# A two-layer encoder: accumulating transfers for low parts, one later mean, x in four transfers with a reordered first norm

## The chip, the cores and the metric

One core of a Trainium2 chip runs the whole kernel. The metric is the device time of one execution in microseconds, from the first instruction to the last and what lies around them. The time before the change is 1551.14 us, the median of three runs (1551.08 to 1551.52).

The engines are TensorE (PE in the rows; PEld is its loading of weights), VectorE (DVE), ScalarE (ACT), GpSimd (POOL) and SyncE (SP), which here only issues transfers. ACTq and SPq are the queues on which ScalarE and SyncE issue transfers; POOL issues some as well, by instructions of its own.

## The reference

Two equal layers work on 512 tokens of 1024 values in float32; 256 memory tokens stand beside them.

```
mem_n = rms_norm(mem, mem_norm_g)
for l in range(DEPTH):                       # 2
    h = rms_norm(x, g_pre_mix[l])
    proj = h @ w_in[l]                       # 1024 -> 5632, split in q, k, v of three branches, and gates
    o_a = neighborhood_attention(q_a, k_a, v_a, rpb_na[l])   # a learned position bias
    o_b = dilated_attention(q_b, k_b, v_b)
    o_m = memory_attention(q_m, mem_n, w_mem_kv[l])
    merged = sum over the branches of sigmoid(gate + b_gate[l]) * (o @ w_br[l])
    x = x + rms_norm(merged @ w_out[l], g_post_mix[l])
    h = rms_norm(x, g_pre_ffn[l])
    a, b = split(depthwise_conv(h @ w_up[l]))
    x = x + rms_norm((gelu(a) * b) @ w_down[l], g_post_ffn[l])
```

## The kernel before

Activations stand with the channels on the 128 partitions and the tokens in the columns: x is eight tiles of 128 channels (k = 0 to 7), each in two halves of 256 tokens. Every float32 matrix product is made from three products of rounded numbers: a number is split into a high part (its value rounded to the type that TensorE takes at full rate) and a low part (what is left), and `mm3` adds high x high, high x low and low x high. So each weight that is loaded (`wraw`, by SP, 512 KB for a column of 1024 x 128) is turned into a high part by a cast on ScalarE and a low part by a subtraction on VectorE or POOL (`split`, L223 to L225). In the groups that this change is about, high and low parts are tiles `m` of 128x512, two of each for a column of weights. There are three raw buffers, so a load waits until the one three before it has been read.

The program of TensorE is written by a scheduler (`Woven`): jobs are generators that say with `yield` by how much work of TensorE their next step comes later, and TensorE's instructions go out in that order. The other engines get their instructions in the order in which the steps are run, and each engine works through its own list in order. So a `yield`, or the time at which a job is spawned, sets the place of all that the job issues, on every engine.

A norm is made by `rstd_job`: TensorE multiplies squares by a column of 1/1024 (`pt<-mean,...`, the mean), ScalarE takes a square root, VectorE the reciprocal, and TensorE spreads it over the partitions (`pt<-ident,st`). Then `normed` makes h for each k on VectorE (`h<-x,g,pt`), ScalarE casts its high part and VectorE subtracts the low part.

The start. x comes in eight transfers of 256 KB on SP; TensorE runs two products with zeros meanwhile (`idle(2)`). ScalarE squares half 0 (y<-x), VectorE adds the squares in pairs, four means follow, then h of half 0. The first six columns of w_in, the groups, are worked in pairs by `run_group`, half 0 first: pairs of groups 0 and 1 (`mm<-h,m`), 2 and 3 (`o` and `pt`), 4 and 5 (`s<-h,m x48`: eight k, three products, two groups), then the same for half 1. The low parts of groups 0, 1, 2 and 4 are VectorE's, those of 3 and 5 POOL's. The norm of half 1 is spawned at SD1 = 4.0 and that of the memory tokens (`mem_norm_job`: four loads `in_memT` on ScalarE's queue, squares on ScalarE) at 6.0. POOL also loads the position bias of a head (128 KB, `in_rpb`, into a `y` buffer) and subtracts it from three masks (`a_bias`, L596 and L599).

The passage from layer 0 to layer 1. While the last products of layer 0 end, `end_job` adds the normed result to x for half 0 (VectorE: y<-y,pt, then x<-x,y) and squares it (ScalarE: sq, VectorE: acc<-acc,sq), and the mean of acc gives layer 1 its first norm. `raw_end_job` does this for half 1, whose groups are multiplied with x before its norm is known; its own mean of squares comes 3.5 of TensorE's time after the last step. `kv_ahead` splits the weights for the keys and values of the memory (KVE, four columns) and of the first two groups (GEN[0], GEN[1]); the other four groups follow. In GEN and KVE, V is VectorE and G is POOL.

Of the kernel before, what the change touches and what calls it, by code (L numbers as in the profile page):

```python
# [37 lines left out]
SQG, LOG, GEN, KVE = {0: (), 1: ()}, {0: (), 1: ()}, 'GGVGVG', 'VVGG'  # L38
SD1 = 4.0
# [80 lines left out]
def tile_hybrid_encoder(ctx, tc, xT, memT, memg, vecs, rpb, w_in, w_kv, w_bra, w_brb, w_brm,  # L120
# [59 lines left out]
    DUP, MDUP = G, G  # L180
    MSQ = G
# [10 lines left out]
    def load_x(half):  # L192
        for k in range(0, KD, 2):
            i = half.start // 256
            nc.sync.dma_start(out=xs[:, i, k:k + 2, :], in_=xT[:, i, k:k + 2, :])
# [31 lines left out]
    def weights(src, K, C, slot=None, eng=None, after=None):  # L227

        raw = wp.tile([128, K, C], F32, tag="wraw", name=nm("wraw"))
        nc.sync.dma_start(out=raw, in_=src)  # L230
        if slot is None:
            hi = wp.tile([128, K, C], F32R, tag="whi", name=nm("whi"), bufs=2)
            lo = wp.tile([128, K, C], F32R, tag="wlo", name=nm("wlo"), bufs=2)
            split(raw, hi, lo, eng)
            behind(last_copy[0], after)
            return [(hi[:, k, :], lo[:, k, :]) for k in range(K)]
        n = 512 // C
        w = []
        for k in range(0, K, n):
            c = min(n, K - k)  # L240
            hi, lo = slot(F32R, (128, c, C)), slot(F32R, (128, c, C))
            split(raw[:, k:k + c, :], hi, lo, eng)
            w += [(hi[:, i, :], lo[:, i, :]) for i in range(c)]
        return w
# [81 lines left out]
    def rstd_job(accs, n, box):  # L326
# [4 lines left out]
        for i, a in enumerate(accs):  # L331
            for b in range(nb):
                mm(pt[:, b:b + 1], a[:, 128 * b:128 * b + 128], mean, i == 0 and b == 0,
                   i == len(accs) - 1 and b == nb - 1, 0.11)
        rs = smalls(nb)
        crit[0] = ACT.activation(rs, pt, AF.Sqrt, bias=eps, scale=1.0).ins
        V.reciprocal(rs, rs)
        yield 0.8
        for b in range(nb):
            one = rs[:, b:b + 1]  # L340
            spread = bass.AP(one.tensor, one.offset, [list(one.ap[0]), [0, 128]])
            wv.pe(nc.tensor.transpose(pr[:, 128 * b:128 * b + 128], spread, ident), 0.11)
        box.append(pr)
# [20 lines left out]
    def pre_norm_job(l, goff, acc, hs, i):  # L364
        half, box = HALVES[i], []
        yield from rstd_job(acc if isinstance(acc, list) else [acc[:, half]], 256, box)
# [51 lines left out]
    def raw_end_job(l, goff, og, acc, acc2, nxt, lat):  # L418
# [17 lines left out]
        yield 3.5  # L436
# [428 lines left out]
    def first_squares(half):  # L865
        sqs = [ytile((128, 256)) for _ in range(KD)]
        for k in range(KD):
            ACT.activation(sqs[k], xh(k, half), AF.Square)
# [8 lines left out]
    def idle(n):  # L877

        one, none = mean[:, 0:1], zero[:, 0:1]
        a, b = (bass.AP(t.tensor, t.offset, [list(t.ap[0]), [0, w]]) for t, w in ((one, 128), (none, 512)))  # L880
        for _ in range(n):
            mm(idle_bank, a, b, True, True, 0.0)
# [3 lines left out]
    wv.spawn(pre_norm_job(0, V_PRE, first_squares(HALVES[0]), hs, 0))  # L886
    gw = group_weights([w_in[0, m] for m in FIRST[:2]], (V, V))
# [7 lines left out]
    gw += group_weights([w_in[0, m] for m in FIRST[2:]], (V, G, V, G))  # L895
# [6 lines left out]
    for l in range(depth):  # L902
# [99 lines left out]
        else:  # L1002
# [10 lines left out]
            def kv_ahead(l=l, pre=pre, gw=gw):  # L1013
                pre.append(weights(w_kv[l + 1, 0], KD, 128, htile))
                yield KVD
                for i in (1, 2, 3):
                    yield 0.9
                    pre.append(weights(w_kv[l + 1, i], KD, 128, big, G if KVE[i] == 'G' else V))
                wv.give(f"kv{l + 1}")
                for m in range(NG):  # L1020
                    yield GWD
                    gw.extend(group_weights([w_in[l + 1, FIRST[m]]], [G if GEN[m] == 'G' else V]))
# [6 lines left out]
            gw += group_weights([w_in[l + 1, m] for m in FIRST[NG:]], [G if e == 'G' else V for e in GEN[NG:]])  # L1029
# [34 lines left out]
def _layout(inputs):  # L1064
# [13 lines left out]
    a["xT"] = np.ascontiguousarray(g["x"][0].T.reshape(KD, 128, 2, 256).transpose(1, 2, 0, 3))  # L1078
# [46 lines left out]
```

## Time and profile before

| | before |
|---|---|
| median of three runs | 1551.14 us |
| the profiled execution | 1551.73 us |
| its span, first to last instruction | 1550.0 us |
| TensorE busy | 1522.5 us (98%) |
| VectorE, ScalarE, POOL busy | 951.6, 712.7, 149.7 us |
| mean granted clock of TensorE | 0.995 |

All rows come from one profiled execution. The page gives the whole; TensorE's idle time is span less busy time. The list of waits says what TensorE waited for and on whom; the timeline shows one line for a run of equal instructions on an engine, with its start, duration and count, and in brackets the idle time before it and what ended it. The granted clock is the share of TensorE's full speed, 1.00 for 2.4 GHz and 0.50 for 1.2 GHz.

### The profile page before, as it was taken

To read this page: it belongs to the slowest core of one execution; us is meant where nothing else is said; L and a number is where in the kernel's file an instruction comes from. 1 tells how busy PE (TensorE), PEld (TensorE's weight loads), DVE (VectorE), ACT (ScalarE), POOL (GpSimd) and SP (SyncE) were. 2 spreads that over 40 slices of the span, in tenths; PEclk is the share of its full clock that TensorE was granted. 3 is DMA by queue.
4 is the path that set the end of the run, shared out by engine and by line. 5 is a ranking of instruction groups with operands and counts; after the bars stand their busy time and mean duration, and the time that the engine had idled before them with its cause. 6 is when DMAs were issued, how large, how long until landed. Compare 5 with 4: busy or idle time off the path is not lost.

```text
span 1550.0 us, 20648 instructions
## 1 busy us (share of the span) xinstructions
PE 1522.5 (98%) x7970; PEld 1300.1 (84%) x7970; DVE 951.6 (61%) x1684; ACT 712.7 (46%) x1266; POOL 149.7 (10%) x217
## 2 busy tenths in 40 slices
PE   8999999999999999999989999999999999999997
PEld 7988888888988888888888888888889888888887
DVE  6685676335777777742497756753456977776233
ACT  5565554336544444532355555532354544444231
POOL 3340000110000000000154300002100000000000
PEclk9999999999999999999999999999999999999999
DMA  7221213235113322333431221132350233323331
GB/s 246 89 88 64 62 57 107 84 95 165 53 59 100 100 96 95 118 90 101 129 102 59 78 66 58 61 104 88 102 177 15 82 96 99 101 99 89 99 105 63
DMA packets 45810, 144.91 MB, mean 93 GB/s; under 512 B 5376, under 2 KB 9600, under 8 KB 45712
## 3 DMA queue, kind: packets, MB, share of 16 engines
q1 hardware_dynamic: 43776, 139.85, 28.5%
q10 hardware_dynamic: 1296, 2.10, 0.4%
q0 software_dynamic: 640, 1.64, 0.3%
q8 instruction: 62, 1.02, 0.3%
q14 instruction: 36, 0.29, 0.1%
HBM read 141.48 MB, written 2.10 MB: 93 GB/s over the span
## 4 chain that ended last, share of the span: by engine, by line
PE 91%; DVE 6%; ACT 2%; issue 1%; DMA 0%; SPq 0%; ACTq 0%; DVEq 0%
PE mm L247 80%; PE s L247 4%; PE o L247 3%; PE pt L258 2%; DVE m L114 1%; DVE y L114 1%; PE pt L247 1%; DVE ka L114 1%; DVE x L114 1%; ACT y L114 1%; DVE st L114 0%; DVE acc L114 0%; DMA x<-in_xT_dram 0%; DVE wlo L114 0%; ACT whi L114 0%
## 5 line engine op out<-in xcount | busy, mean ns | idle before, releaser
L247 PE MATMUL mm<-h,whi 128*128 128x512 f32 x2496 | 776.5, 392 | 0.0
L247 PEld LDWEIGHTS mm<-h,whi 128*128 128x128 f32 x2496 | 462.0, 188 | 91.3
L247 PE MATMUL mm<-h,wlo 128*128 128x512 f32 x1248 | 486.9, 390 | 0.0
L114 DVE TENSOR_TENSOR wlo<-wraw,whi 128x1024 fp32r<-128x1024 f32 (+1 forms) x213 | 259.2, 1217 | 284.7 <-ACT whi L114 282.3
L114 ACT CAST whi<-wraw 128x1024 fp32r<-128x1024 f32 (+1 forms) x213 | 221.4, 1040 | 307.8 <-PE mm L247 293.4
L247 PEld LDWEIGHTS mm<-h,wlo 128*128 128x128 f32 x1248 | 234.5, 188 | 49.6
L247 PE MATMUL mm<-m,whi 128*128 128x512 f32 (+1 forms) x800 | 215.1, 356 | 1.0 <-DVE m L114 0.8
L247 PEld LDWEIGHTS mm<-m,whi 128*128 128x128 f32 x800 | 141.8, 189 | 22.8 <-PE mm L247 1.3
L247 PE MATMUL mm<-m,wlo 128*128 128x512 f32 (+1 forms) x400 | 142.1, 355 | 0.0
L114 DVE SCALAR_TENSOR_TENSOR y<-y,vec,y 128x511 f32<-128x511 f32 x176 | 130.5, 748 | 3.5 <-ACT y L114 0.9
L114 DVE TENSOR_TENSOR y<-mm,R 128x512 f32<-128x512 f32 x82 | 56.4, 688 | 68.5 <-PE mm L247 68.5
L247 PEld LDWEIGHTS mm<-m,wlo 128*128 128x128 f32 x400 | 75.5, 189 | 10.9
L802 POOL TENSOR_TENSOR m<-m,y 128x512 f32<-128x512 f32 x28 | 36.1, 1289 | 399.4 <-DVE y L114 399.4
L114 ACT ACTIVATE y<-y,vec 128x512 f32<-128x512 f32 x88 | 71.1, 815 | 2.3 <-DVE y L114 1.9
L247 PE MATMUL mm<-m,m 128*128 128x512 f32 x240 | 63.5, 394 | 0.0
L114 ACT ACTIVATE y<-y 128x512 f32<-128x512 f32 x44 | 27.9, 633 | 71.7 <-DVE y L114 71.3
L114 ACT CAST m<-pt 128x512 fp32r<-128x512 f32 (+1 forms) x72 | 38.6, 541 | 46.8 <-PE pt L258 38.5
L114 ACT ACTIVATE y<-y,st 128x256 f32<-128x256 f32 (+1 forms) x80 | 43.8, 549 | 30.4 <-DVE st L114 28.9
L114 DVE TENSOR_TENSOR acc<-acc,sq 128x256 f32<-128x256 f32 (+1 forms) x80 | 41.1, 514 | 26.6 <-ACT sq L114 24.7
L114 DVE TENSOR_TENSOR m<-pt,m 128x512 fp32r<-128x512 f32 (+1 forms) x72 | 45.1, 630 | 19.9 <-ACT m L114 18.6
L114 ACT CAST m<-y 128x512 fp32r<-128x512 f32 x32 | 19.9, 622 | 72.5 <-DVE y L114 72.5
L247 PE MATMUL mm<-h,m 128*128 128x256 f32 x312 | 49.1, 301 | 2.0 <-ACT h L114 1.0
(154 smaller groups left out, 1789.9 us busy)
## 6 DMA issues: line engine op xcount, KB each, us to landing
wraw<-in_w_in_dram SPq DMA_DIRECT2D x88, 512.0 KB, 3.7
wraw<-in_w_up_dram SPq DMA_DIRECT2D x88, 512.0 KB, 3.6
wraw<-in_w_down_dram SPq DMA_DIRECT2D x32, 512.0 KB, 3.5
wraw<-in_w_out_dram SPq DMA_DIRECT2D x16, 512.0 KB, 3.9
wraw<-in_w_down_dram SPq DMA_DIRECT2D x16, 384.0 KB, 3.1
wraw<-in_w_kv_dram SPq DMA_DIRECT2D x8, 512.0 KB, 4.0
wraw<-in_w_bra_dram SPq DMA_DIRECT2D x16, 192.0 KB, 2.3
x<-in_xT_dram SPq DMA_DIRECT2D x8, 256.0 KB, 7.3
```

The lines of the kernel that those rows point to most:

```text
L114: return op(*args, **kw)
L247: wv.pe(nc.tensor.matmul(ps, a, b, start=first, stop=last), cost)
L258: wv.pe(nc.tensor.transpose(ps[:, 128 * i:128 * i + 128], s, ident), 0.11)
L802: (V if br == 2 and m >= 6 else G).tensor_add(acc[m], acc[m], gs)
```

## The change

It has three parts.

First, a third way to make a low part, named D: ScalarE casts the high part as before, then writes minus the rounded value into the low part's tile, and POOL issues a transfer of 256 KB that reads the weight again from memory and adds it to what stands in the tile (L246 of the changed kernel). Sixteen tiles are made so: those of groups 4 and 5 in layer 0 (POOL had 3 and 5), and of the key-value columns 2 and 3 and groups 0, 1, 4 and 5 in layer 1 (POOL had the two columns, and groups 0, 1, 3 and 5). POOL makes no low parts of weights any more.

Second, the mean of half 1 in `raw_end_job` comes after 5.0 instead of 3.5 of TensorE's time.

Third, x comes in four transfers of 512 KB, 4 KB per partition. In the first norm VectorE makes two of the eight squares, `rstd_job` puts four short products with zeros between its steps (one after the second mean, one before the spreading, two behind it), the second group's weights are split after the norm's job is spawned, and SD1 becomes 5.0.

```diff
-SQG, LOG, GEN, KVE = {0: (), 1: ()}, {0: (), 1: ()}, 'GGVGVG', 'VVGG'
-SD1 = 4.0
+SQG, LOG, GEN, KVE = {0: (), 1: ()}, {0: (), 1: ()}, 'DDVVDD', 'VVDD'
+SD1 = 5.0
...
+    ENG = {'G': G, 'V': V, 'D': 'D'}
...
     def load_x(half):
-        for k in range(0, KD, 2):
+        for k in range(0, KD, 4):
             i = half.start // 256
-            nc.sync.dma_start(out=xs[:, i, k:k + 2, :], in_=xT[:, i, k:k + 2, :])
+            nc.sync.dma_start(out=xs[:, i, k:k + 4, :], in_=xT[i, k // 4])
...
             hi, lo = slot(F32R, (128, c, C)), slot(F32R, (128, c, C))
-            split(raw[:, k:k + c, :], hi, lo, eng)
+            if eng == "D":
+                last_copy[0] = ACT.copy(hi, raw[:, k:k + c, :]).ins
+                ACT.activation(lo, raw[:, k:k + c, :], AF.Copy, scale=-1.0)
+                nc.gpsimd.dma_start(out=lo, in_=src[:, k:k + c, :], accum_op=ALU.add)
+            else:
+                split(raw[:, k:k + c, :], hi, lo, eng)
...
-    def rstd_job(accs, n, box):
+    def rstd_job(accs, n, box, warm=None):
...
+            if warm and i == 1:
+                warm(1, 256)
         rs = smalls(nb)
         crit[0] = ACT.activation(rs, pt, AF.Sqrt, bias=eps, scale=1.0).ins
         V.reciprocal(rs, rs)
+        if warm:
+            warm(1, 256)
         yield 0.8
...
+        if warm:
+            warm(2, 256)
         box.append(pr)
...
-        yield 3.5
+        yield 5.0
...
-            ACT.activation(sqs[k], xh(k, half), AF.Square)
+            if half == HALVES[0] and k in (3, 7):
+                V.tensor_mul(sqs[k], xh(k, half), xh(k, half))
+            else:
+                ACT.activation(sqs[k], xh(k, half), AF.Square)
...
-    def idle(n):
+    def idle(n, w=512):
...
-    wv.spawn(pre_norm_job(0, V_PRE, first_squares(HALVES[0]), hs, 0))
-    gw = group_weights([w_in[0, m] for m in FIRST[:2]], (V, V))
+    sqs = first_squares(HALVES[0])
+    gw = group_weights([w_in[0, FIRST[0]]], (V,))
+    wv.spawn(pre_norm_job(0, V_PRE, sqs, hs, 0, idle))
+    gw += group_weights([w_in[0, FIRST[1]]], (V,))
...
-    gw += group_weights([w_in[0, m] for m in FIRST[2:]], (V, G, V, G))
+    gw += group_weights([w_in[0, m] for m in FIRST[2:]], (V, V, 'D', 'D'))
```

The change moves instructions at three places.

ScalarE at the start, from the split of group 5 (before, `m_274` and `m_278`; after, `m_276` to `m_282`): casts of h's second half (`h<-h`), loads of the memory tokens and their squares. Before:

```order
L114 CAST m_278<-wraw_272 128x512
L114 CAST h_116<-h_85_363 128x256
L455 DMA m_387<-in_memT_dram 128x512
L114 CAST h_118<-h_86_367 128x256
...
L114 CAST h_124<-h_89_379 128x256
L114 CAST h_126<-h_90_383 128x256
L455 DMA m_393<-in_memT_dram 128x512
L114 ACTIVATE h_95_395<-m_387 128x256
```

After:

```order
L114 ACTIVATE m_282<-wraw_274 128x512
L467 DMA m_357<-in_memT_dram 128x512
...
L467 DMA m_363<-in_memT_dram 128x512
L114 ACTIVATE h_87_365<-m_357 128x256
...
L114 ACTIVATE sq_93_382<-m_363 128x256
L114 CAST h_110<-h_95_396 128x256
...
L114 CAST whi_706<-wraw_704 128x1024
L114 CAST whi_747<-wraw_745 128x1024
L114 CAST h_114<-h_97_404 128x256
```

The memory tokens' loads and squares have moved from behind the casts of h to ahead of them, and two casts of 128x1024 stand among the casts of h.

POOL at the start, from the first work on groups: the splits of groups 3 and 5 before, the accumulating transfers of groups 4 and 5 after, and the bias loads of two heads with their subtractions. Before:

```order
L225 TENSOR_TENSOR m_255<-wraw_252,m_254 128x512
L225 TENSOR_TENSOR m_259<-wraw_252,m_258 128x512
L225 TENSOR_TENSOR m_275<-wraw_272,m_274 128x512
L225 TENSOR_TENSOR m_279<-wraw_272,m_278 128x512
L596 DMA y_925<-in_rpb_dram 128x256
L599 TENSOR_TENSOR y_924<-mask,y_925 128x256 x2
```

After:

```order
L608 DMA y_929<-in_rpb_dram 128x256
L611 TENSOR_TENSOR y_928<-mask,y_929 128x256 x2
L611 TENSOR_TENSOR y_929<-mask,y_929 128x256
L246 DMA m_265<-in_w_in_dram 128x512
L608 DMA y_1012<-in_rpb_dram 128x256
L246 DMA m_270<-in_w_in_dram 128x512
L246 DMA m_277<-in_w_in_dram 128x512
L246 DMA m_282<-in_w_in_dram 128x512
```

The work on the groups stood ahead of the first bias load; now it stands behind that load and its three subtractions, and a second bias load stands inside it.

POOL between the layers, groups 3 and 5 before, 4 and 5 after. Before:

```order
L225 TENSOR_TENSOR m_7249<-wraw_7242,m_7248 128x512
L225 TENSOR_TENSOR m_7265<-wraw_7262,m_7264 128x512
L225 TENSOR_TENSOR m_7269<-wraw_7262,m_7268 128x512
L596 DMA y_7760<-in_rpb_dram 128x256
L599 TENSOR_TENSOR y_7759<-mask,y_7760 128x256 x2
```

After:

```order
L608 DMA y_7776<-in_rpb_dram 128x256
L246 DMA m_7267<-in_w_in_dram 128x512
L246 DMA m_7272<-in_w_in_dram 128x512
L611 TENSOR_TENSOR y_7775<-mask,y_7776 128x256 x2
L246 DMA m_7279<-in_w_in_dram 128x512
L611 TENSOR_TENSOR y_7776<-mask,y_7776 128x256
L246 DMA m_7284<-in_w_in_dram 128x512
```

The bias load has moved ahead of the groups' work, and two subtractions stand between group 4's transfers and group 5's.

## Rows read from the trace of the kernel before

**Rows 1.** The page: the span, and part 1 (busy time, share, instructions)
```profile
span 1550.0 us, 20648 instructions
...
PE 1522.5 (98%) x7970; PEld 1300.1 (84%) x7970; DVE 951.6 (61%) x1684; ACT 712.7 (46%) x1266; POOL 149.7 (10%) x217
```

**Rows 2.** What TensorE waited for: us in total, times, longest
```profile
PE pt L247 <- DVE acc L114: 4.6, 2, 3.5
PE pt L247 <- DVE y L114: 3.2, 4, 2.0
```

**Rows 3.** Timeline, 0 to 46 us (columns: start, duration, engine, ...)
```profile
0.95 3.78 PE L247 MATMUL o<-zero,mean 128*128 128x512 f32 x4 [0.95 <-POOL zero L206]
...
5.88 0.72 ACT L114 ACTIVATE y<-x 128x256 f32<-128x256 f32 x2 [0.47 <-DMA x<-in_xT_dram]
...
8.88 0.72 ACT L114 ACTIVATE y<-x 128x256 f32<-128x256 f32 x2 [2.27 <-DMA x<-in_xT_dram]
...
10.12 1.01 PE L247 MATMUL pt<-mean,y 128*128 128x1 f32 x4 [1.98 <-DVE y L114]
...
12.41 0.48 DVE L114 SCALAR_TENSOR_TENSOR h<-x,g,pt 128x256 f32<-128x256 f32 x1 [0.78 <-PE pt L342]
12.81 0.68 DVE L114 TENSOR_TENSOR m<-wraw,m 128x512 fp32r<-128x512 f32 x1
...
20.95 0.42 DVE L114 TENSOR_TENSOR h<-h,h 128x256 fp32r<-128x256 f32 x1
...
31.23 5.92 PE L247 MATMUL s<-h,m 128*128 128x256 f32 x48
...
42.40 0.96 PE L247 MATMUL mm<-h,m 128*128 128x256 f32 x6
```

**Rows 4.** Timeline of the passage between the layers, 766 to 816 us
```profile
770.41 2.22 DVE L114 TENSOR_TENSOR x<-x,y 128x256 f32<-128x256 f32 x2
...
779.65 1.83 DVE L114 TENSOR_TENSOR x<-x,y 128x256 f32<-128x256 f32 x2
...
783.59 0.58 PE L247 MATMUL pt<-mean,acc 128*128 128x1 f32 x4 [3.46 <-DVE acc L114]
...
786.10 4.79 PE L247 MATMUL mm<-h,m 128*128 128x256 f32 x30
...
799.41 0.41 DVE L114 TENSOR_TENSOR x<-x,y 128x256 f32<-128x256 f32 x1
...
804.44 5.92 PE L247 MATMUL s<-h,m 128*128 128x256 f32 x48
```

**Rows 5.** Timeline of POOL and ScalarE's queue, 28 to 41 us
```profile
28.90 2.91 POOL L225 TENSOR_TENSOR m<-wraw,m 128x512 fp32r<-128x512 f32 x2 [2.08 <-ACT m L114]
...
31.76 0.61 POOL L596 DMA_DIRECT2D y<-in_rpb_dram  x1
...
33.25 0.33 ACTq L455 DMA_DIRECT2D m<-in_memT_dram  x1
...
38.85 2.32 POOL L599 TENSOR_TENSOR y<-mask,y 128x256 f32<-128x256 f32 x3 [6.48 <-DVE h L114]
```

**Rows 6.** Page, part 5: costliest groups (busy, mean ns of one)
```profile
L114 DVE TENSOR_TENSOR wlo<-wraw,whi 128x1024 fp32r<-128x1024 f32 (+1 forms) x213 | 259.2, 1217 | 284.7 <-ACT whi L114 282.3
L114 ACT CAST whi<-wraw 128x1024 fp32r<-128x1024 f32 (+1 forms) x213 | 221.4, 1040 | 307.8 <-PE mm L247 293.4
...
L114 ACT CAST m<-pt 128x512 fp32r<-128x512 f32 (+1 forms) x72 | 38.6, 541 | 46.8 <-PE pt L258 38.5
```

**Rows 7.** Loads by tile: the bias, the memory tokens, w_in, in this order
```profile
DMA to landing us min/median/max: 2.3/2.9/7.0
...
DMA to landing us min/median/max: 3.2/5.5/6.1
...
DMA to landing us min/median/max: 3.4/3.7/8.3
```

**Rows 8.** One stretch behind the mean at 783.59: busy times, clock, DMA
```profile
784.80:788.20 3.40, 3.30 (x17) 3.01 (x16) 2.97 (x9) 1.64 (x5) 2.29 (x6) 0.50 0.02 5
```

More of the change, by code (lines that the diff above doesn't have):

```diff
@@ L362, in scaled, with pre_norm_job @@
         return y
-    def pre_norm_job(l, goff, acc, hs, i):
+    def pre_norm_job(l, goff, acc, hs, i, warm=None):
         half, box = HALVES[i], []
-        yield from rstd_job(acc if isinstance(acc, list) else [acc[:, half]], 256, box)
+        yield from rstd_job(acc if isinstance(acc, list) else [acc[:, half]], 256, box, warm)
         for k in range(KD):
@@ L875, in tile_hybrid_encoder @@
     idle_bank = obank(128)
-    def idle(n):
+    def idle(n, w=512):
         one, none = mean[:, 0:1], zero[:, 0:1]
-        a, b = (bass.AP(t.tensor, t.offset, [list(t.ap[0]), [0, w]]) for t, w in ((one, 128), (none, 512)))
+        a, b = (bass.AP(t.tensor, t.offset, [list(t.ap[0]), [0, w]]) for t, w in ((one, 128), (none, w)))
         for _ in range(n):
-            mm(idle_bank, a, b, True, True, 0.0)
+            mm(idle_bank[:, 0:w], a, b, True, True, 0.0)
     idle(2)
     hs = h_tiles()
-    wv.spawn(pre_norm_job(0, V_PRE, first_squares(HALVES[0]), hs, 0))
-    gw = group_weights([w_in[0, m] for m in FIRST[:2]], (V, V))
+    sqs = first_squares(HALVES[0])
+    gw = group_weights([w_in[0, FIRST[0]]], (V,))
+    wv.spawn(pre_norm_job(0, V_PRE, sqs, hs, 0, idle))
+    gw += group_weights([w_in[0, FIRST[1]]], (V,))
     load_x(HALVES[1])
@@ L1017, in kv_ahead @@
                     yield 0.9
-                    pre.append(weights(w_kv[l + 1, i], KD, 128, big, G if KVE[i] == 'G' else V))
+                    pre.append(weights(w_kv[l + 1, i], KD, 128, big, ENG[KVE[i]]))
                 wv.give(f"kv{l + 1}")
@@ L1021, in kv_ahead @@
                     yield GWD
-                    gw.extend(group_weights([w_in[l + 1, FIRST[m]]], [G if GEN[m] == 'G' else V]))
+                    gw.extend(group_weights([w_in[l + 1, FIRST[m]]], [ENG[GEN[m]]]))
                 wv.give(f"gw{l + 1}")
@@ L1028, in tile_hybrid_encoder @@
             wv.need(f"gw{l + 1}")
-            gw += group_weights([w_in[l + 1, m] for m in FIRST[NG:]], [G if e == 'G' else V for e in GEN[NG:]])
+            gw += group_weights([w_in[l + 1, m] for m in FIRST[NG:]], [ENG[e] for e in GEN[NG:]])
             wv.need(f"h{l + 1}.{V_PRE}.0")
@@ L1077, in _layout @@
     a = {}
[L1078 removed]
+    a["xT"] = np.ascontiguousarray(g["x"][0].T.reshape(2, 4, 128, 2, 256).transpose(3, 0, 2, 1, 4))
     a["memT"] = np.ascontiguousarray(g["mem"][0].T.reshape(KD, 128, N_MEM).transpose(1, 0, 2))
```

## Prediction

> **What bounds the kernel now.** The page gives the span and TensorE's busy share [rows 1]: with 98% busy, only some 27 us of the 1550 are not TensorE work, and a change that touches no matmul of the body can only win or lose in those holes. Next comes the list of what TensorE waited for [rows 2]: about 8 us of it are the norms' means, which wait for sums of squares. The change touches two stretches, so I read these in the timeline: the first 45 us [rows 3] and the passage from layer 0 to layer 1 at 768 to 815 us [rows 4]. In the first the reader is to see a chain: x lands, is squared, averaged, and VectorE makes h; TensorE then goes from group to group. In the second the reader is to see a mean (783.59) that waits 3.46 us for VectorE's sums, with POOL's splits beside them. Everywhere else TensorE is full, and what it loses before it is not given back.
>
> **The start, x and the first norm.** The fourth 256 KB of x are waited for until 8.88 today [rows 3]. Two transfers of 512 KB should land by about 6.0 (the third 256 KB are there at 5.88); bounds 5 and 8.9. Even so, TensorE does not follow at once: its two idle products last until 4.73, each of the four means takes 1.01, and one fill matmul, 0.95 (a quarter of 3.78), stands among them: 4.73 + 4 x 1.02 + 0.95 plus small gaps is 10.2, against 11.13 today. Square root and reciprocal end at 10.7, the second fill at 11.15, two transposes take 0.7: h's first product starts at 11.9 instead of 12.41. VectorE's two squares lie in the time in which x lands and cost nothing; if x came as late as today they would still be done before it. From 11.9 on VectorE makes eight h's with four weight splits between them instead of five (0.68 each), so h is done at 21.37 - 0.5 - 0.68 = 20.2, and TensorE, which follows h, is **1.2 us ahead**. It reaches the pair of groups 4 and 5 at 30.0 instead of 31.23.
>
> **The start, the accumulating transfers.** Their four low parts were POOL's, four splits of about 1.45 [rows 5], the last done at 31.81. Now ScalarE makes eight passes of 0.55 (as a cast [rows 6]) and POOL issues. But on POOL they now stand behind the first bias load and its three mask subtractions. That load's buffer held a square of half 1 and comes free when VectorE has summed it; those sums follow h, so about 21.5. Its landing took 7.0 in this stretch today and 2.3 to 4.2 elsewhere [rows 7]; I take 3.5, hence 25.0; the subtractions take 2.32 [rows 5], so POOL is free at 27.3. One issue takes 0.6 [rows 5]; the order is transfer, bias load, two transfers, so the third transfer, the first half of group 5, is issued at 27.3 + 3 x 0.6 = 29.1. An accumulating transfer is nowhere in this trace. Nearest below is the 128 KB bias load, 2.3 and 2.9; nearest above are 7.0 for it here and 8.3 for a weight load [rows 7]. A 512 KB weight load takes 3.7 as a rule [rows 7], so 256 KB that are read and added on a busy stretch I put at 4.5; bounds 2.3 and 7.0. It lands at 33.6. TensorE needs it in the pair's sixth matmul, at 30.0 + 0.6: **a wait of 3.0**. After a wait of 3.46 the clock was granted at 0.50, the lower of its levels, 1.2 GHz [rows 8]; 30 matmuls then took 4.79, where 48 take 5.92 at the full clock [rows 4], so 1.1, and some 0.4 more on their neighbours: 1.5 in all. The pair ends at 33.6 + 43 x 0.123 + 1.5 = 40.4 instead of 31.23 + 5.92 = 37.15: **+3.3**.
>
> A second claim on the same stretch: ScalarE now has the memory tokens' loads and squares ahead of the casts of h's second half. Today those casts were over when it waited for the last such load, issued 33.25 [rows 5]. ScalarE's eight passes should be through at about 28.2 (four more than today's casts, without the casts of h that stood between), and four issues of 0.33 follow. The last load is thus issued at 29.2 and lands after 5.5 to 6.1, the upper part of its range [rows 7], at 34.7 to 35.3. Behind it come two squares and eight casts of 0.4 and two weight casts of 1.04, with VectorE's two weight splits of 1.22 and eight low parts of h between them [rows 6]; some 9.4, and 0.7 for TensorE's last matmuls: groups 0 and 1 end for half 1 at 45.1 instead of 43.36 [rows 3]. This is +1.7, less than the +3.3 already there, so it hides behind it, but it is a floor if the transfers are quick. From memory loads at 3.2 it would be -0.9.
>
> **Between the layers.** Twelve POOL splits go, eight of them in 768 to 781. A pair of VectorE's additions x<-x,y takes 2.22 beside them (the first of such places, at 770.41; the last, at 779.65, 1.83) and 0.41 each alone [rows 4]; six such places, additions and sums, lose 5.3 us together. The last sum is then ready at 778.9 or so, not 783.59; TensorE arrives at 780.13 and does not wait. The 3.46 go, and with them the 1.5 at the half clock: **5.0 earlier**. The later mean of half 1 removes the other wait on sums, 4.6 - 3.5 = **1.1** [rows 2]; its 14 matmuls of cover are there today, only behind it.
>
> But the pair of groups 4 and 5, today at 804.44, is then reached at 799.4 and needs its third transfer at 800.0. On POOL this stands behind the bias load and two mask subtractions. The load's buffer comes free with VectorE's addition at 799.41 + 0.41 [rows 4], 5.0 for the advance and some 0.7 for POOL's absence earlier: 794.1. It lands after 2.3 to 4.2 (3.2), two subtractions at 0.77, a third of 2.32, follow, and the transfer is issued at 798.9. Here the queues are quieter; I take a weight load's 3.7, bounds 2.3 and 4.5: it lands at 802.6, **a wait of 2.6**, and since that is shorter than the 3.46 behind which the clock fell, half of the 1.5. Net: 5.0 + 1.1 - 2.6 - 0.75 = **2.75 gained**. The first two groups and the last key-value parts have a lead of 5 us or more, so their transfers cost nothing; without that cover each would cost its landing. The 4 MB read twice I cost at nothing: TensorE waits for no load in [rows 2].
>
> **Sum.** +3.3 - 2.75 = +0.55. The profiled execution took 1551.73 (span 1550.0); the median of the runs is 1551.14, 0.6 less. On the median: **1551.7**. No change, then, and 0.2% of it, 3.1 us, is what a measurement of this kernel can tell.
>
> A page of the Trainium skill gives another price. The bias load's shortest landing is 2.3 for 128 KB [rows 7]. "DMA: Bandwidth & Descriptors", section "Anatomy of one DMA — SWDGE (gpsimd) path", gives a fixed 2.0 us and the bytes at 436 GB/s: 2.3 for 128 KB, which that shortest one bears out and the 7.0 does not, and 2.6 for 256 KB. By it the waits at both pairs shrink by 1 to 2 us each, and the sum would be about -3.
>
> **Rivals.**
> *Landings as short as the shortest row, 2.3, at both places.* At the start the third transfer is issued at 27.6 (when ScalarE has the copies) and there at 29.9: no wait; the memory loads' floor of +1.4 to +1.7 is left. Between the layers it is there at 800.3: a wait of 0.3, a gain of 5.8. Sum -4.4: 1546.7; with memory loads at 3.2, 1544.4. For it: three of the landings named were 2.3 to 2.9. Against: these loads are half the size and only write.
>
> *Landings as long as the longest, 7.0, at the start.* The bias load issued at 31.76 had its subtraction at 38.85 [rows 5], while VectorE worked almost without a gap. Then POOL is free at 30.8, the transfer is issued at 32.6 and lands at 39.6; the pair ends at 46.4, +9.2, and with 2.75 back the kernel is at 1557.6, **slower**. It decides from the point where the two landings in a row take 2.5 more than my 8.0. If they were 7.0 between the layers too, the time would be near 1566; the landings there today speak against it.
> The Trainium skill has a mechanism for it: "SBUF — State Buffer", section "SBUF: two separate sides", says that transfers issued from GpSimd starve for descriptors while VectorE holds the port that the two share. By that rule the start, where VectorE makes h, would give the long landing; the trace agrees at 31.76 with its 7.0, but not at the passage, where VectorE was as busy and a landing took 2.3.
>
> *The mean's wait stays,* because ScalarE, with sixteen more passes, gives the squares late: of the 5.0 only 2 come, TensorE reaches the pair 3 later, and the wait there goes instead. Net gain near 1 to 2: 1552 to 1553, which is the forecast again; if the first two groups' transfers come late as well, 1555. The change then doesn't do what it says.
>
> **Chances.** Forecast, no measurable change: 0.45, its own range 1548 to 1554.5. Short landings: 0.23. Long landings: 0.27. The mean's wait with late transfers: 0.05. Faster 0.23, same 0.45, slower 0.32. The range runs from 1546.0 to 1558.5: it leaves out the memory loads at their shortest and the long landings at both places.
>
> **What would show it.** Right: x's squares unbroken before 7 us; h's first product near 11.9; a TensorE wait of about 3 near 30 to 34 on a transfer issued by POOL, and the half clock after it; casts of h's second half behind the memory squares; no wait at the mean near 780; a wait of 2 to 3 at the pair near 800; the accumulating transfers' landing of 3.5 to 4.5. Wrong: a landing under 3 or over 6, a bias load that goes much earlier or later than 21.5, or VectorE's sums that stay slow without POOL's splits.

## The result and the profile after

The changed kernel takes 1559.85 us (median of four runs, 1559.13 to 1561.05) beside 1551.33 for the kernel before on the same chip: a ratio of 1.0052, 95% interval 1.0035 to 1.0070. It is 8.5 us slower, outside the range that was forecast, 1546.0 to 1558.5, by 1.35. The profiled execution has a span of 1558.3, 8.3 more than before.

The page and the list of TensorE's waits, after:

```profile
span 1558.3 us, 20682 instructions
...
PE 1526.3 (98%) x7978; PEld 1303.7 (84%) x7978; DVE 942.3 (60%) x1686; ACT 717.5 (46%) x1280; POOL 143.0 (9%) x217
```

```profile
PE s L253 <- DMA m<-in_w_in_dram: 11.5, 4, 5.1
PE pt L253 <- DVE y L114: 2.2, 2, 1.1
...
PE mm L253 <- DMA m<-in_w_in_dram: 1.3, 1, 1.3
```

The waits on means for VectorE's sums, 4.6 [rows 2], are gone from the list. In their place stand 11.5 us of waits for a transfer that writes `m` from w_in: accumulating transfers. TensorE's busy time is 3.8 higher, but not with work: the eight new records are the four fill products at the start, and products at the lower clock are busy for longer.

Where the 8.6 us came in is read from TensorE's marks, the starts of the same instruction in both traces (the n-th `pt<-mean` or `s<-ka` of the program):

| mark | before | after minus before |
|---|---|---|
| mean of half 1, layer 0 | 23.54 | -1.43 |
| mean of the memory tokens | 42.03 | +9.40 |
| last mean of layer 0's products | 767.81 | +9.39 |
| mean of half 0 at the passage | 783.59 | +5.77 |
| next mean of half 1 | 794.16 | +5.57 |
| mean of half 1's squares (the later one) | 813.64 | +12.21 |
| attention, 10 us on | 823.61 | +10.69 |
| attention | 877.74 | +8.56 |
| last mean of the kernel | 1539.38 | +8.58 |

So the start lost 9.4, of which nothing came back in 720 us; the passage first gave 3.8 back, then lost 6.6, and gave back 1.5 and 2.1: -0.8 net. The timeline of the start after:

```profile
4.63 1.03 ACT L114 ACTIVATE y<-x 128x256 f32<-128x256 f32 x3 [1.96 <-DMA x<-in_xT_dram]
...
5.88 1.03 ACT L114 ACTIVATE y<-x 128x256 f32<-128x256 f32 x3 [0.21 <-DMA x<-in_xT_dram]
...
11.58 1.91 PE L253 MATMUL o<-zero,mean 128*128 128x256 f32 x4
11.82 0.48 DVE L114 SCALAR_TENSOR_TENSOR h<-x,g,pt 128x256 f32<-128x256 f32 x1
...
20.77 0.61 POOL L608 DMA_DIRECT2D y<-in_rpb_dram  x1 [7.67 <-DVE y L114]
...
22.11 1.05 PE L253 MATMUL pt<-mean,y 128*128 128x1 f32 x8 [1.06 <-DVE y L114]
...
27.23 0.92 POOL L246 DMA_DIRECT2D m<-in_w_in_dram  x1
...
28.38 3.02 POOL L246 DMA_DIRECT2D m<-in_w_in_dram  x3
...
30.60 0.40 PE L253 MATMUL s<-h,m 128*128 128x256 f32 x2
...
34.98 0.42 ACT L114 ACTIVATE sq<-m 128x256 f32<-128x256 f32 x1 [1.75 <-DMA m<-in_memT_dram]
35.30 0.39 ACT L114 CAST h<-h 128x256 fp32r<-128x256 f32 x1
...
36.08 1.01 PE L253 MATMUL s<-h,m 128*128 128x256 f32 x3 [5.08 <-DMA m<-in_w_in_dram]
...
38.85 7.71 PE L253 MATMUL s<-h,m 128*128 128x256 f32 x43 [1.75 <-DMA m<-in_w_in_dram]
```

x is squared from 4.63 and 5.88 with a gap of only 0.21, h begins at 11.82 and the mean of half 1 stands at 22.11: all of this near the forecast. The memory tokens' last load is waited for until 34.98, and the first cast of h's second half stands behind it at 35.30. But TensorE, which had reached the pair of groups 4 and 5 at 30.60, waits 5.08 and then 1.75 more for the transfers that POOL issued at 27.23 and 28.38 to 29.48, and behind the wait its 43 matmuls take 7.71 instead of 43 x 0.123 = 5.3. The transfers that end the two waits are the first and the third: they land at 36.03 and 38.80. The landings of all sixteen transfers, from issue to landing:

```profile
DMA to landing us min/median/max: 4.4/9.1/11.1
```

Three stretches after (from and to, length, then the busy time of TensorE, its weight loads, VectorE, ScalarE and POOL with the number of instructions; the last three columns are the granted clock, the transfer engines' busy share and GB/s):

```profile
24.00:40.00 16.00, 9.16 (x55) 8.67 (x55) 6.86 (x14) 9.73 (x21) 8.93 (x11) 0.71 0.90 241
27.20:36.00 8.80, 3.80 (x32) 3.59 (x30) 1.98 (x5) 3.61 (x11) 4.20 (x6) 0.88 0.99 287
768.00:790.00 22.00, 22.00 (x187) 22.00 (x186) 13.69 (x34) 16.54 (x39) 7.08 (x9) 1.00 0.70 186
```

Two of them before:

```profile
24.00:40.00 16.00, 16.00 (x136) 16.00 (x136) 10.61 (x26) 8.85 (x23) 7.33 (x7) 1.00 0.63 208
768.00:790.00 22.00, 18.44 (x141) 17.97 (x142) 18.71 (x38) 10.97 (x29) 14.26 (x16) 0.92 0.38 120
```

The median landing is 9.1 us, the forecast had 4.5 and 3.7. From the first issue to the first landing, 27.2 to 36.0, the transfer engines are 99% busy, and over 24 to 40 their share has gone from 63% to 90%, at 768 to 790 from 38% to 70%. The passage, after:

```profile
779.81 0.75 DVE L114 TENSOR_TENSOR x<-x,y 128x256 f32<-128x256 f32 x2
...
789.36 0.50 PE L253 MATMUL pt<-mean,acc 128*128 128x1 f32 x4
...
798.07 1.82 PE L253 MATMUL mm<-h,m 128*128 128x256 f32 x13 [1.31 <-DMA m<-in_w_in_dram]
...
803.34 0.57 POOL L608 DMA_DIRECT2D y<-in_rpb_dram  x1 [10.09 <-DVE x L114]
...
808.69 2.52 POOL L611 TENSOR_TENSOR y<-mask,y 128x256 f32<-128x256 f32 x2 [3.00 <-DVE ka L114]
...
809.90 0.40 PE L253 MATMUL s<-h,m 128*128 128x256 f32 x2
...
810.98 0.62 PE L253 MATMUL s<-h,m 128*128 128x256 f32 x3 [0.68 <-DMA m<-in_w_in_dram]
...
811.15 0.87 POOL L246 DMA_DIRECT2D m<-in_w_in_dram  x1
...
815.60 6.87 PE L253 MATMUL s<-h,m 128*128 128x256 f32 x43 [4.00 <-DMA m<-in_w_in_dram]
```

VectorE's pair of additions takes 0.75 now instead of 2.22 [rows 4], the mean at 789.36 waits for nothing, and TensorE reaches the pair at 809.90, 5.5 later than before, having been 9.4 behind. On the way it waited 1.31 for a transfer of the first two groups (the row at 798.07). At the pair it waits 0.68 and 4.00. The transfer that ends the second wait was issued at 811.15, behind two subtractions that began at 808.69, when the bias load of 803.34 had landed.

### The profile page after: what moved, and what is told of

Its sections match the earlier page's. It is cut to its first block, busy times and chain, and to the rows that moved or that the text cites. A ratio compares the mean times of both kernels' runs of the same rounds, so it can differ in the third digit from the quotient of the medians.

```text
span 1558.3 us, 20682 instructions
## 1 busy us (share of the span) xinstructions
PE 1526.3 (98%) x7978; PEld 1303.7 (84%) x7978; DVE 942.3 (60%) x1686; ACT 717.5 (46%) x1280; POOL 143.0 (9%) x217
## 4 chain that ended last, share of the span: by engine, by line
PE 91%; DVE 4%; DMA 2%; ACT 1%; issue 1%; POOL 0%; POOLq 0%; ACTq 0%
PE mm L253 80%; PE s L253 5%; PE o L253 3%; PE pt L264 2%; DMA m<-in_w_in_dram 2%; DVE y L114 1%; DVE m L114 1%; PE pt L253 1%; DVE ka L114 1%; DVE x L114 0%; DVE h L114 0%; ACT whi L114 0%; DVE wlo L114 0%; ACT y L114 0%; DVE st L114 0%
## 5 line engine op out<-in xcount | busy, mean ns | idle before, releaser
L253 PE MATMUL s<-h,m 128*128 128x256 f32 x336 | 51.8, 303 | 11.5 <-DMA m<-in_w_in_dram 11.5
L253 PEld LDWEIGHTS s<-h,m 128*128 128x128 f32 x336 | 47.0, 209 | 12.4 <-DMA m<-in_w_in_dram 12.4
L114 DVE TENSOR_TENSOR acc<-acc,sq 128x256 f32<-128x256 f32 (+1 forms) x80 | 38.4, 480 | 29.1 <-ACT sq L114 27.4
```

Of the source, the lines that this page charges most:

```text
L114: return op(*args, **kw)
L253: wv.pe(nc.tensor.matmul(ps, a, b, start=first, stop=last), cost)
```

## The experiments

Two things could explain the start: the transfers, or the memory tokens' squares ahead of h's casts. And a late landing could be the transfer's own price, its place on POOL, or the sharing of the transfer engines. All the ratios are against runs of the kernel before on the same chip. In the table, "start" is the shift of the mark at 42.03, "passage" what is added between 767.81 and the kernel's last mean, both from each run's one profiled execution; landings are minimum, median and maximum of the transfers that POOL issues for low parts. The timed runs were 4 to 12 of each kernel; e10 and e13 have one run each and no ratio.

| run | ratio, 95% interval | start | passage | landings |
|---|---|---|---|---|
| changed kernel | 1.0052 (1.0035 to 1.0070) | +9.4 | -0.8 | 4.4/9.1/11.1 |
| e1, no transfers | 1.0017 (1.0007 to 1.0027) | +2.6 | -1.5 | none |
| e2, start only | 1.0050 (1.0032 to 1.0067) | +8.8 | -2.5 | 8.3/9.4/10.3 |
| e3, passage only | 1.0041 (1.0026 to 1.0057) | +3.7 | +0.6 | 4.6/9.6/11.7 |
| e4, plain transfers | 1.0027 (1.0016 to 1.0038) | +6.3 | -2.9 | 3.6/5.8/8.2 |
| e5, bias behind | 1.0054 (1.0038 to 1.0070) | +5.7 | 0.0 | 7.4/9.7/11.2 |
| e6, h first | 1.0068 (1.0054 to 1.0082) | +8.2 | +2.7 | 5.4/9.6/11.4 |
| e7, both | 1.0068 (1.0055 to 1.0082) | +9.4 | +2.3 | 6.5/9.8/13.4 |
| e8, no transfers, h first | 0.9993 (0.9984 to 1.0002) | +1.1 | -2.2 | none |
| e9, key-value loads later | 1.0056 (1.0041 to 1.0072) | +6.3 | -1.1 | 4.1/9.3/11.2 |
| e11, mean only | 0.9990 (0.9981 to 0.9999) | -0.2 | -2.7 | none |
| e12, x only | 0.9997 (0.9989 to 1.0006) | -1.6 | +0.7 | none |
| e14, mean and x | 0.9986 (0.9977 to 0.9995) | +0.4 | -3.5 | none |
| e15, half the transfers | 1.0029 (1.0020 to 1.0038) | +4.5 | -2.4 | 7.8/8.2/8.7 |

In these runs the kernel before took between 1547.8 and 1554.7, a wider spread than in the four runs above; between the profiled executions of kernels whose starts are the same program the start differs by 1.2 us (e1, e3, e10 and e13) and by 2.1 (e12 and e14). So differences of up to 2 us between single profiles are not read below. The trace of the kernel before is that of an execution of 1551.73, 0.8 to 1.9 above its medians beside the experiments, so the two columns can read too low: in e9 they add up to 5.2, where its timed runs lose some 8.

**Which part loses: e1, e2, e3.** Against the changed kernel (here and below, the remark behind a line names the runs that have it):

```diff
-SQG, LOG, GEN, KVE = {0: (), 1: ()}, {0: (), 1: ()}, 'DDVVDD', 'VVDD'
+SQG, LOG, GEN, KVE = {0: (), 1: ()}, {0: (), 1: ()}, 'GGVGVG', 'VVGG'   # e1, e2
...
-    gw += group_weights([w_in[0, m] for m in FIRST[2:]], (V, V, 'D', 'D'))
+    gw += group_weights([w_in[0, m] for m in FIRST[2:]], (V, G, V, G))   # e1, e3
```

> The changed kernel without accumulating transfers: low parts by VectorE and POOL as in the kernel before, with x in four transfers, the reordered first norm and the later mean kept. If the whole loss is TensorE's wait on the transfers, the start keeps the 1.4 us by which TensorE was ahead at the mean of half 1, the later mean keeps about 1.5, and the time is about 1548.5 (ratio 0.998). Rival: the loss at the start comes from the memory tokens' loads and squares that stand ahead of the casts of h's second half; they stay ahead here, so the start would still lose 2 us or more and the time would be 1553 or above.

> Accumulating transfers for groups 4 and 5 of layer 0 alone; between the layers low parts by VectorE and POOL as before. If the start's four transfers cost 9.4 us, as the shift of TensorE's marks says, and the passage is as before but for the later mean, about 1559 to 1559.5; the 3.46 us wait at the mean of half 0 is back. Rival, that the loss is shared between the two places: about 1555.

> Accumulating transfers between the layers alone; groups 3 and 5 of layer 0 split on POOL as before. If the passage is a small gain of 0.8 us net (an advance of 3.9, a wait and half clock of 6.7, the later mean's 1.5 and 2.1 more later) and the start keeps its 1.4: about 1549. Rival, loss shared: about 1555.

The start with transfers (e2) costs 8.8, that without (e1) 2.6: the transfers are the larger part, some 6 us, but not all of it. The prediction's floor, the memory tokens ahead of h, is there when they are gone. In e1 the timeline shows it:

```profile
32.23 0.42 ACT L114 ACTIVATE sq<-m 128x256 f32<-128x256 f32 x1 [1.00 <-DMA m<-in_memT_dram]
32.56 0.39 ACT L114 CAST h<-h 128x256 fp32r<-128x256 f32 x1
...
33.47 2.00 ACT L114 CAST whi<-wraw 128x1024 fp32r<-128x1024 f32 x2
...
34.33 1.75 PE L253 MATMUL mm<-h,m 128*128 128x256 f32 x12
...
36.47 0.40 ACT L114 CAST h<-h 128x256 fp32r<-128x256 f32 x1 [1.01 <-DVE h L114]
...
36.93 0.38 PE L253 MATMUL mm<-h,m 128*128 128x256 f32 x1 [0.85 <-ACT h L114]
...
38.69 2.93 PE L253 MATMUL mm<-h,m 128*128 128x256 f32 x12 [1.38 <-DVE h L114]
...
42.27 2.48 PE L253 MATMUL mm<-h,m 128*128 128x256 f32 x17 [0.65 <-DVE h L114]
```

TensorE begins the pair for half 1 at 34.33, but the squares of the last memory load hold ScalarE until 32.56, one cast of h and two weight casts follow, and the next casts of h come from 36.47 on, behind VectorE. It waits 0.85, 1.38 and 0.65 there. My expectation for e1 (1548.5) was wrong and its rival right; e2 came near its expectation (1558.64), and e3 was worse than its own (1557.68 instead of 1549), for the most part because its start is that of e1. Between the layers the sum of gains and waits is about nothing (+0.6 in e3), while POOL's splits, with the later mean, give -1.5 and -2.5 (e1, e2). The timed runs agree that the transfers gain nothing there over POOL's splits: e3 is 0.24% above e1, and the changed kernel 0.02% above e2.

**Is it the adding: e4.** The same transfers without the addition:

```diff
-nc.gpsimd.dma_start(out=lo, in_=src[:, k:k + c, :], accum_op=ALU.add)
+nc.gpsimd.dma_start(out=lo, in_=src[:, k:k + c, :])
```

> The changed kernel with plain transfers in place of the accumulating ones, same bytes, same queue, same order; the low parts then hold the weight itself instead of the remainder, so the addition is left out. Theory: adding holds the transfer engines about twice as long per byte as writing. Then landings fall from a median of 9.1 to about 5, the start loses about 4 instead of 9.4, and the time is 1553 to 1554.5. Rival: the landings are late because the memory tokens' loads and the key-value weights go at the same time, or because of the queue on POOL; then they stay at 8 to 10 at the start and the time stays at 1558 or above.

Between theory and rival: the ratio is 1.0027, about half of the loss, and the passage gains 2.9. But at the start plain transfers still land after 7.6 to 8.2. Adding has a price of its own, seen in the time that the packets of each queue took, as a share of 16 engines, in 27 to 41 us (packets, MB, share). First the changed kernel:

```profile
q0 software_dynamic: 624, 1.18, 44.8%
q1 hardware_dynamic: 292, 1.06, 20.7%
q10 hardware_dynamic: 479, 0.86, 20.1%
```

The run with plain transfers:

```profile
q1 hardware_dynamic: 359, 1.32, 28.5%
q0 software_dynamic: 624, 1.18, 26.1%
q10 hardware_dynamic: 494, 0.88, 18.9%
```

The software queue moved the same 1.18 MB in both, in 44.8% of the engines' time when it added and 26.1% when it only wrote: 1.7 times as much for each byte. In that stretch it is 6.3 instead of 3.7 us of all sixteen engines. (A plain bias load of 0.13 MB is in both.)

**Is it the place on POOL or the order on ScalarE: e5, e6, e7.**

```diff
-nc.gpsimd.dma_start(out=lo, in_=src[:, k:k + c, :], accum_op=ALU.add)
+last_lo[G] = nc.gpsimd.dma_start(out=lo, in_=src[:, k:k + c, :], accum_op=ALU.add).ins   # e5, e7
-SD1 = 5.0
+SD1 = 4.00                       # e6, e7
```

> The changed kernel with one line more: each accumulating transfer counts as POOL's last low part, so that the bias load is put behind the transfers again, at the start and between the layers. If the place behind the bias load is what makes the transfers late, they are issued 2 to 3 us earlier at the start and 5 earlier for group 5 between the layers; the start loses about 7 instead of 9.4 and the wait of 4.0 at 815 goes to about 2: 1554 to 1556 in all (ratio 1.002 to 1.003). Rival: how long they take to land is set by the load of the transfer engines in the stretch; then an earlier issue lands hardly earlier and the time stays at 1558 or above.

> The changed kernel with SD1 = 4.0 as before, which on ScalarE puts the casts of h's second half ahead of the memory tokens' loads and squares again; transfers untouched. Theory: with the transfers in place TensorE is behind anyway, so the order on ScalarE is hidden and the start still loses 8 to 9.4: 1558.5 to 1559.9. The memory tokens' 1 MB are loaded later, which may let the transfers land 1 to 3 us earlier: down to 1557. Rival, the order is the main cause: 1554.5.

> Both of the former: bias load behind the transfers, and SD1 = 4.0. The transfers go out ahead of the memory tokens' loads and of the bias load. If issue time and shared transfer engines add up, they land near 32 to 34, the start loses 3 to 4, and the time is near 1550 to 1552. If the key-value weights that are loaded at the same time suffice to hold them up, the start still loses 6 or more: 1555.

In e5 the transfers of the start are issued from 22.98 on instead of 27.23, 3.4 to 4.4 earlier, and the last lands at 37.24 instead of 40.14, each after 8.9 to 11.2; but in this profile TensorE and the memory tokens' loads stood about 2 us earlier too, so little of the +5.7 is the order's. Between the layers group 5's are issued at 801.6 and 802.6 and take 9.4 and 9.7 where they took 4.4 and 4.7. The timed runs show no gain, 1.0054, against an expectation of 1.002 to 1.003: this order does not mend it. e6 and e7 came out slower than their expectations (1561.63 and 1561.82; 1555 at most was expected of e7). In them ScalarE issues the memory tokens' last load at 29.97 and 30.91 instead of 25.87; it lands at 38.7 and 41.8 instead of 34.9, and the last transfer at 39.95 and, although issued 1.3 earlier than in the changed kernel, at 41.62. Both ratios are 1.0068, higher than the changed kernel's, with intervals that overlap its own. So neither order carries the loss: what is sent earlier is not landed earlier by as much, and what is sent beside it lands later. That points to a sum of bytes.

**Without transfers, h first: e8.** e1's engines with SD1 = 4.00.

> No accumulating transfers at all, and SD1 = 4.0: x in four transfers, the reordered first norm and the later mean alone. The run without transfers lost 2.5 us by the mark at 42 us although TensorE was 2.8 ahead at 22, because TensorE waited for casts of h behind the memory tokens' squares. If that order is the cause, the 2.8 stay, and with the 1.5 of the later mean the time is about 1547 (ratio 0.997). If not, it equals the run without transfers, 1.0017.

It is 0.9993, not clear of 1, where 0.997 was expected, and 0.24% below e1: the order on ScalarE costs 3 to 4 us when no transfer hides it. The 2.8 by which TensorE was ahead at the mean do not stay, though; at 42 us it is 1.1 behind. The traces show where the 3.9 go. The mean of half 1 takes 1.4 longer, its second part waiting 0.80, and the matmuls from there to the pair take 9.3 instead of 6.8, because the clock is at its lower level for a part of them. The stretch before, in e8, and in e11, whose start is that of the kernel before:

```profile
22.00:32.00 10.00, 9.14 (x77) 8.94 (x76) 8.10 (x19) 7.31 (x18) 5.81 (x5) 1.00 0.55 178
22.00:32.00 10.00, 9.86 (x58) 9.86 (x59) 7.09 (x19) 5.61 (x14) 4.35 (x4) 0.66 0.65 197
22.00:32.00 10.00, 10.00 (x72) 10.00 (x73) 7.68 (x19) 5.96 (x14) 6.17 (x5) 0.83 0.64 184
```

TensorE had waited 2.01 and 0.80 at the mean in e8 and 1.47 in e11; in the kernel before it waited 0.86, and the granted clock was 1.00. e11 has no part of the change before 768 us; yet it was ahead by 1.65 at the mean (its fourth load of x was there at 7.27 instead of 8.88) and by 0.15 at 42 us. So such a lead comes without the change as well, and goes again at the lower clock.

**What shares the engines: e9, e15, e10, e13.** e9 lets POOL issue the key-value loads; e15 makes group 5 alone by transfers, and takes the first line of e1 and e2 besides:

```diff
-def weights(src, K, C, slot=None, eng=None, after=None):
+def weights(src, K, C, slot=None, eng=None, after=None, q=None):   # e9
...
-        nc.sync.dma_start(out=raw, in_=src)
+        (q or nc.sync).dma_start(out=raw, in_=src)   # e9
...
-w = pre[m] if pre else weights(w_kv[l, m], KD, 128)
+w = pre[m] if pre else weights(w_kv[l, m], KD, 128, q=G)      # e9
...
-    gw += group_weights([w_in[0, m] for m in FIRST[2:]], (V, V, 'D', 'D'))
+    gw += group_weights([w_in[0, m] for m in FIRST[2:]], (V, V, V, 'D'))   # e15
```

> The changed kernel with the four 512 KB loads of layer 0's key-value weights issued by POOL, in its order: one ahead of the accumulating transfers, three behind them, instead of all on SyncE from 23.6 us on. Theory: the transfers land late because the transfer engines are shared with what is loaded beside them. With 1.0 to 1.5 MB less beside them they land after 6 to 8 instead of 8.8 to 10.7, and the start loses 6 to 7.5 instead of 9.4. Rival: four accumulating transfers take this long whatever is beside them; then landings stay at 9 to 10 and the start at 9.4 or above.

> Accumulating transfers for group 5 of layer 0 alone (two instead of four at the start, none between the layers). If the transfer engines are the limit there, half a megabyte less lets the last one land 2 to 3 us earlier than the 39.1 of the run with four, and the start loses 5.5 to 7 instead of 8.8. If the price is one of each transfer, the landing stays at 9 to 10 after issue and the start loses 8 or more.

e9 settles little. The transfers still take 8.8 to 9.7. The loads behind them were issued by POOL at 28.25 and 28.80, against 25.57 and 27.64 in the changed kernel, so they ran beside the transfers after all. The start's +6.3 goes with an issue at 24.6 instead of 27.2, but the timed runs, 1.0056, show no gain. In e15 the two transfers land after 7.8 and 8.7, at 33.7 and 35.2, where the run with four had its last at 39.1; the start loses 4.5 instead of 8.8, with a wait of 4.1. Of the 3.9 by which the last lands earlier, 2.3 are an earlier issue (26.50 instead of 28.79) and 1.6 a shorter landing. Less is lost than I had expected; a sum of bytes would give the 1.6, but e15 alone does not show it.

Both of the next are e1 with one column of w_up in each layer made by transfers: e10 at 377 us, e13 a column whose load stands before a pause, at 412:

```diff
-                     ms, 4, (V_PREF, hs, R), fill=[lambda m=m: gw.extend(group_weights([w_up[l, m]], (V,))) for m in up])
+                     ms, 4, (V_PREF, hs, R), fill=[lambda m=m: gw.extend(group_weights([w_up[l, m]], ('D' if m == 1 else V,))) for m in up])   # e10
...
-        ahead = [weights(w_up[l, rest[0]], KD, 128)]
+        ahead = [weights(w_up[l, rest[0]], KD, 128, big, 'D')]   # e13
```

> The run without transfers, with one column of w_up in each layer (two tiles, near 420 and 1190 us, where the transfer engines are busy 4 to 10%) made by accumulating transfers. It measures the price alone. If an accumulating transfer of 256 KB by itself costs what the last two between the layers showed, 3.8 to 4.8 from issue to landing; if the late landings are its own price, 7 or more. The time is not expected to move.

> The run without transfers, with one column of w_up whose load at 412 us is followed by some 25 us without any other load made by two accumulating transfers. If the late landings come from sharing the transfer engines, they land after 3.5 to 5 here. If 7 to 9 is what accumulating transfers take anyway, 7 or more.

e10 missed its aim: the place was not quiet, four loads of 512 KB went beside the two transfers, which landed after 7.3 and 8.7 (7.7 and 9.1 in layer 1). The stretch from the first issue to the first landing in e10:

```profile
376.60:383.90 7.30, 7.30 (x34) 6.05 (x33) 3.03 (x4) 3.85 (x7) 1.81 (x2) 1.00 0.87 218
```

e13 has both cases side by side. Its issues, the two stretches from issue to landing, and the landings of both layers:

```profile
412.04 0.93 POOL L246 DMA_DIRECT2D m<-in_w_up_dram  x1 [55.17 <-ACT m L114]
...
414.24 1.31 SPq L231 DMA_DIRECT2D wraw<-in_w_up_dram  x2
...
414.51 0.89 POOL L246 DMA_DIRECT2D m<-in_w_up_dram  x1 [1.54 <-ACT m L114]
```

```profile
412.00:416.00 4.00, 4.00 (x36) 4.00 (x35) 3.92 (x10) 4.00 (x12) 1.82 (x2) 1.00 0.54 87
414.50:422.40 7.90, 7.90 (x69) 7.90 (x68) 7.53 (x20) 4.62 (x15) 0.89 (x1) 1.00 0.71 186
```

```profile
DMA to landing us min/median/max: 4.0/5.5/7.9
```

The first transfer goes alone until 414.24 and lands after 4.0, in layer 1 too. The ScalarE passes freed the raw buffer, two loads of 512 KB went out at 414.24 and 415.22, and the second transfer, issued at 414.51 beside them, took 7.9 (6.9 in layer 1); the loads took 5.3 and 7.4, where 3.6 is the median. The second had another transfer of its own queue ahead of it until 416.05, which is a rival reason for its 7.9. The first transfer of e10 had none, only loads beside it, and took 7.3: company is enough. Nearly alone an accumulating transfer has about the price that I had forecast; in company it has nearly twice that, and its companions take 1.5 to 2 times as long.

**The parts that cost nothing: e11, e12, e14.** The kernel before with `yield 5.0` (e11), with x in four transfers (e12), with both (e14).

> The kernel before with the later mean alone (5.0 instead of 3.5). The wait of 1.1 us at that mean should go, and the loss of some 2 us at 873 (a wait and the half clock behind it) went in every run that had the later mean: 1549 to 1550.3 (ratio 0.9987 to 0.9995). Rival: only the wait goes somewhere else: 1551, no difference.

> The kernel before with x in four transfers alone, the first norm and its order untouched but for what the scheduler makes of it: on ScalarE two more weight casts now stand ahead of the casts of h. x lands by 6 instead of 8.9, but TensorE at the half clock sets the means: gain of at most 0.5 to 1 us, ratio 0.9993 to 1.000. Rival: the moved weight casts hold up h, 1.0005 or more.

> The kernel before with the later mean and x in four transfers, nothing else of the change. Alone the first measured 0.9990 and the second 0.9997; added up 0.9987, with the interval clear of 1. Rival: the gains meet in the same later wait and do not add: 0.9995.

All three came as expected. e14, 0.9986, has the lowest ratio here and is clear of the kernel before, by about 2 us, though not clear of e11. By its profile the gain lies between the layers: 1.5 at the later mean, and the rest in the stretch at 873, where TensorE before waited 2.09 and then ran at the half clock. In the changed kernel, e1, e11 and e14 it waits 1.6 to 2.1 there, the clock stays up, and 1.5 to 2.1 us less are lost. This second part is not tied to the mean: in e5, e6 and e7, with the same later mean, the clock fell there as well (0.79 over the 8 us around it), and in e12, without it, it stayed at 1.00.

## Why the prediction was wrong

The forecast was 1551.7, no change; 1559.85 was measured. Its rival of long landings gave 1557.6 with a chance of 0.27, and by place and kind that is what happened: +9.2 for the start, +9.4 measured. That the sums agree so well is luck. The rival had two landings of 7.0 in a row, the bias load's and the transfer's; measured were 4.3 and 9.9, which add up to nearly the same.

**The step that failed** is the landing of an accumulating transfer, "256 KB that are read and added on a busy stretch I put at 4.5; bounds 2.3 and 7.0", and 3.7 between the layers. Measured: 8.8 to 10.7 at the start, 6.8 to 11.1 for the key-value parts and the first groups, 7.0 and 9.4 for group 4 of layer 1 and 4.4 and 4.7 for its group 5. The value of 4.5 is near that of a transfer alone (4.0 in e13). A landing over 6 was one of the prediction's own signs of being wrong. What I left out is that landings were taken from rows in which the engines had room, 63% busy at 24 to 40 us before, while the change itself fills them: 1 MB more, at 1.7 times the engine time for each byte (e4), and loads that start earlier. The third key-value load goes out at 27.64 instead of 31.83, because ScalarE frees the raw buffer that POOL held before, and the memory tokens' last load at 25.87 instead of 33.25, by its new place on ScalarE. I had put the second reading of 4 MB at nothing, since TensorE waited for no load; with the engines at 99% it is paid for, by the transfers, by the memory tokens (9.0 instead of 6.1 for the slowest load) and by the second bias load (8.5).

The other steps, measured: x at 4.6 and 5.9 (6.0 forecast), h from 11.82 (11.9), ahead by 1.43 at the mean (1.2), bias load at 20.77 (21.5), POOL free at 27.2 (27.3), third transfer issued at 28.94 (29.1): right by number. For h and the lead at the mean this is luck in part: over all runs with this first norm h begins anywhere from 10.0 to 12.1, and e11, which has none of it, begins h at 10.79. Of the lead 0.6 was left at the pair (30.60; 30.0 forecast): the granted clock was 0.83 over 22 to 32 us, a fall that the forecast did not have. An issue takes 0.9 to 1.9, not 0.6. The waits at the pair were 6.8 instead of 3.0, and the half clock cost 2.4 on the 43 matmuls instead of 1.5 in all. The memory tokens' chain was hidden, as said, and as a floor it was 2.6 (e1; 1.7 forecast). Their last load landed at 34.9, as forecast, but by two errors that cancel: it was issued at 25.87 (29.2) and took 9.0 (5.5 to 6.1).

Between the layers the mechanism was right and three terms too small. Of the advance of 5.0, 3.8 came: the mean's wait went, but the first groups' transfers, "a lead of 5 us or more", landed after 10 us and were waited for (1.3). Group 5's transfer was issued at 811.15, where the forecast's 798.9 and the 9.4 lost at the start make 808.3, since the bias load took 5.2 (3.2) and two subtractions 2.5 (1.55); the waits were 4.7 (2.6) and the half clock 1.6 (0.75). The later mean gave 1.5 (1.1). The 2.1 at 873 I had not foreseen; whether the clock falls there is not tied to the change (it fell in e5 to e7). Sum -0.8 instead of -2.75.

The rival's mechanism, that VectorE's work starves a transfer issued by POOL, is not what these runs show: the long landings at the start fell in 27.2 to 36.0, with VectorE busy 1.98 of 8.80 us, and the short one of e13 in a stretch where it was busy 3.92 of 4.00. The prediction also misread the kernel before there: VectorE did not work almost without a gap behind the bias load of 31.76, but 4.5 of 6.9 us. And the Trainium skill, "SBUF — State Buffer", section "SBUF: two separate sides", says this only of VectorE operations in a two-port mode, which a float32 copy within SBUF triggers. VectorE's rows in these stretches are TENSOR_TENSOR and SCALAR_TENSOR_TENSOR and no copies, so these stretches do not test the rule for copies. The price from the Trainium skill, "DMA: Bandwidth & Descriptors", section "Anatomy of one DMA — SWDGE (gpsimd) path", 2.6 us for 256 KB, is not borne out: the shortest plain transfer took 3.6 (e4), and one that adds, nearly alone, 4.0 (e13).

What stays open: whether the reordered first norm and x in four transfers gain anything at all, since e12 is at 0.9997 and a lead as large comes and goes without them (e11), and how much of the better profiles of e5 and e9 is real, since their timed runs do not show it.

## What to carry to other kernels

A transfer that takes over an engine's work is not priced by landings of today's trace: add its bytes, at what an accumulating byte holds the engines, to the busy share of the stretch in which it lands, and add what starts earlier because a buffer is freed sooner. If that passes the stretch, everything in it lands late, and moving an issue ahead gives little. And a line that lets one instruction follow another by name (here the bias load behind POOL's last low part) silently stops holding when that instruction moves to another engine: look for it in the order. Here it cost little (e5).

## What the runs showed of the hardware

- A transfer that adds holds the transfer engines 1.7 times as long for each byte as one that only writes (44.8% against 26.1% for 1.18 MB), and POOL is 0.86 to 0.93 us with one issue, 0.53 to 0.57 with a plain one, up to 1.9 where issues follow at once.
- 256 KB added nearly alone land after 4.0 (e13, in both layers); beside loads of 512 KB, with no other transfer of POOL's ahead, after 7.3 (e10). Two such loads beside an adding transfer took 5.3 and 7.4 instead of 3.6 (e13).
- At the passage VectorE's additions went from 2.22 to 0.75 for a pair when POOL's subtractions beside them were gone (0.75 in e3 as well, 2.21 in e1 and e2, where the subtractions are back); POOL's issuing of transfers did not slow them.
- Waits of about 2 us of TensorE at the same place of the program (871 before) were followed by the half clock in some profiles (2.09 before, 1.94 in e5) and not in others (1.86 in e1, 2.05 in e11).
